# Softmax sums by transposes and a row reduction instead of products with a matrix of ones

## Chip, core and metric

The kernel runs on one core of a Trainium2 chip. The metric is the device time in microseconds of one execution, as the median of several runs. Below, PE is the matrix engine, DVE the vector engine, ACT the scalar engine, POOL the fourth compute engine and SP the queue that starts most transfers. SBUF is the on-chip working memory, PSUM the smaller memory into which PE writes.

## The reference, cut to what matters

One decoder block over 1024 tokens of 1024 features, all in float32: a norm, an input projection, attention with eight heads of 64 beside a state-space mixer, a gated sum of both, and a mixture of 32 experts. The change is in the attention alone:

```python
logits = jnp.einsum('bhqd,bhkd->bhqk', qb, kf) + cb[..., :, None] - cum[:, :, None, :]
causal = pos[None, :] <= pb[:, None]
logits = jnp.where(causal, logits, NEG_INF)
p = jax.nn.softmax(logits, axis=-1)
return jnp.einsum('bhqk,bhkd->bhqd', p, vf)
```

The softmax is computed as exponentials, their product with the values, and at the end a division by the sum of the exponentials over the keys. The change is in how that sum and its reciprocal are made.

## The kernel before

Work on float32 is done by splitting each operand into a high part that PE multiplies at full speed (type fp32r) and the rest, and adding up three products. The stages follow one another: input and state-space projections (0 to 335 us), attention (335 to 655 us), mixing and output projection, routing, and from about 840 us on the experts.

Attention goes by four pairs of heads. For a pair, `proj` (L783) makes queries, keys and values for one half of the tokens, `prep` (L815) turns them and finds row maxima, and `attend(p_, c)` (L871) handles query half `c` (512 queries): for each head `a` of the pair and each block `kt` of 128 keys, PE writes logits with keys on partitions and queries along the columns (L901 to L904), ACT makes the exponentials twice, once rounded to `pH` (L907) and once in full as `pe` (L909), DVE makes the rest `pL` (L910), POOL adds `pe` into `sm` (L912), and PE multiplies both parts with the values into `acc` (L886, L887). `sm` starts as the first block's exponentials. So at the end `sm` is 128 x 512: for each query a column of 128 partial sums, one for each partition. Only blocks up to the diagonal are computed, and the last two blocks of a query half touch only the right 256 columns.

What remains is to add up the 128 partitions and to divide. `sm` is split into `sh` by ACT (L923) and `sl` by DVE (L925). `sel` holds, for each head, a 128 x 128 matrix with ones in that head's 64 columns. Four products of `sel` with `sh` and `sl` of both heads (L930) add up the partitions and leave, in one PSUM tile, the sum of head 0 in partitions 0 to 63 and that of head 1 in 64 to 127. DVE takes the reciprocal in four pieces of 128 columns (L933) and multiplies each with `yu` (L934), which L920 and L921 had brought out of `acc`. Then `yu` is stored (L941), or, for the last half of the last pair, split at once into `yha`, `yla` (L938, L939).

`run_all` (L740) weaves generators by shares: `attend` of the current pair runs beside `proj` and `prep` of the next. For the second half of pair 2 and for pair 3 the filler is `mixed_ssm` (L713), products with the state-space output (L700 to L702), whose results DVE multiplies with gates into `mixS` (L725); ACT makes those gates with another function table (L707), so it loads tables to and fro. The compiler's scheduling layer then sets the order of each engine's queue by its own estimates, so the order of the finished program differs from that of the code; each engine works through its queue in order.

PSUM tiles come from two rings of four: `psA` (`mmtile`, L60), for projections, `acc` and, before, the tile of the sums (except at the last half), and `psB` (`smtile`, L63), for logits, scores and transposes. A tile is taken when the one four places before it in its ring has been read.

Of the kernel before, what the change touches and what calls it, by code (L numbers as in the profile page):

```python
# [10 lines left out]
F32 = mybir.dt.float32  # L11
F32R = mybir.dt.float32r
# [4 lines left out]
ALU = mybir.AluOpType  # L17
AX = mybir.AxisListType

P = 128  # L20
# [22 lines left out]
def hybrid_block(ctx: ExitStack, tc: tile.TileContext, t, out):  # L43

    nc = tc.nc
# [14 lines left out]
    def mmtile():  # L60
        return psA.tile([P, 512], F32, tag="A", name="psA_t")

    def smtile():  # L63
        return psB.tile([P, 512], F32, tag="B", name="psB_t")

    def f32(ap):
        return ap.bitcast(F32)
# [63 lines left out]
    ident = cp.tile([P, P], F32, name="ident")  # L131
# [600 lines left out]
    gev_stack.close()  # L732
    st = ctx.enter_context(ExitStack())
    ap_ = pool(st, "att", 1, side="right")

    sel = ap_.tile([P, 2, P], F32R, name="sel")
    nc.gpsimd.memset(f32(sel), 0.0)
    for a in range(2):
        nc.gpsimd.memset(f32(sel[:, a, a * 64:a * 64 + 64]), 1.0)
    def run_all(*gens):  # L740

        live = [[g, n, lo, hi, 0] for g, n, lo, hi in gens]
# [128 lines left out]
    def attend(p_, c, last=None):  # L871


        nkt = 4 * c + 4
        yu = ap_.tile([P, 512], F32, name="yu", bufs=1)
        sums = []
        for a in range(2):
            kx, qx, ky, qy = p_.KX[a], p_.QX[a, c], p_.KY[a], p_.QY[a, c]

            acc = psA.tile([P, 512], F32, tag="A", name="acc")  # L880
            sm = ap_.tile([P, 512], F32, name="sm", bufs=2)

            def values(kt, o0, n, pH, pL):
                v = p_.V[:, kt, a].rearrange("p a b -> p (a b)")
                o = acc[:, o0:o0 + n]
                nc.tensor.matmul(o, v, pH[:, :n], start=(kt == 0), stop=False)  # L886
                nc.tensor.matmul(o, v, pL[:, :n], start=False, stop=(kt == nkt - 1))  # L887

            late = []
            for kt in range(nkt):  # L890
                ks = slice(kt * P, kt * P + P)
                o0 = max(0, kt * P - c * 512)
                diag = kt >= 4 * c
                if 512 - o0 < 256:
                    o0 -= P
                    d0, dn = 0, 256
                else:
                    d0, dn = 128, 128
                n = 512 - o0
                ps = smtile()  # L900
                nc.tensor.matmul(ps[:, :n], ky[:, ks], qy[:, o0:], start=True, stop=False)  # L901
                if diag:
                    nc.tensor.matmul(ps[:, 0:dn], identb, mask_s[:, d0:d0 + dn], start=False, stop=False)
                nc.tensor.matmul(ps[:, :n], kx[0:68, ks], qx[0:68, o0:], start=False, stop=True)  # L904
                pH = ap_.tile([P, 512], F32R, name="pH", bufs=4)
                pL = ap_.tile([P, 512], F32R, tag="pL", name="pL", bufs=4)
                nc.scalar.activation(pH[:, :n], ps[:, :n], AF.Exp)  # L907
                pe = ap_.tile([P, 512], F32, name="pe", bufs=3) if kt else sm
                nc.scalar.activation(pe[:, :n], ps[:, :n], AF.Exp)  # L909
                nc.vector.tensor_tensor(pL[:, :n], pe[:, :n], f32(pH[:, :n]), ALU.subtract)  # L910
                if kt:
                    nc.gpsimd.tensor_tensor(sm[:, o0:], sm[:, o0:], pe[:, :n], ALU.add)  # L912
                late.append((kt, o0, n, pH, pL))
                if len(late) > 3:
                    values(*late.pop(0))
                yield
            for v in late:
                values(*v)
            orow = slice(a * 64, a * 64 + 64)
            nc.scalar.copy(yu[orow, :], acc[0:64, :])  # L920
            nc.vector.tensor_tensor(yu[orow, :], yu[orow, :], acc[64:128, :], ALU.add)  # L921
            sh = ap_.tile([P, 512], F32R, name="sh", bufs=1)
            nc.scalar.copy(sh, sm)  # L923
            sl = ap_.tile([P, 512], F32R, tag="pL", name="sl", bufs=4)
            nc.vector.tensor_tensor(sl, sm, f32(sh), ALU.subtract)  # L925
            sums += [(a, sh), (a, sl)]
            yield
        ps = smtile() if last is not None else mmtile()
        for j, (a, v) in enumerate(sums):
            nc.tensor.matmul(ps, sel[:, a], v, start=(j == 0), stop=(j == 3))  # L930
        for q in range(4):
            qs = slice(q * P, q * P + P)
            nc.vector.reciprocal(ps[:, qs], ps[:, qs])  # L933
            nc.vector.tensor_tensor(yu[:, qs], ps[:, qs], yu[:, qs], ALU.mult)  # L934
        if last is not None:
            last.append((slot("yha", dt=F32R), slot("yla", dt=F32R)))
            yh, yl = last[-1]
            nc.scalar.copy(yh[:, 512:S], yu)  # L938
            nc.vector.tensor_tensor(yl[:, 512:S], yu, f32(yh[:, 512:S]), ALU.subtract)  # L939
            return  # L940
        nc.gpsimd.dma_start(yaT_d[p_.pr * P:(p_.pr + 1) * P, c * 512:c * 512 + 512], yu)  # L941
# [576 lines left out]
```

## Time and profile before

| | us |
|---|---|
| median of 3 runs | 1182.69 (1181.4 to 1185.41) |
| the profiled execution, its own time | 1180.84 |
| its span, first to last instruction | 1179.2 |
| attention with what is woven in, 340 to 660 | 320.0 |
| PE busy in those 320 us | 306.3 |
| DVE busy | 271.0 |
| ACT busy | 220.6 |
| POOL busy | 168.2 |

PE's busy time is the union of its instructions' durations. Matmuls overlap, so a matmul's duration (0.39 us for 512 columns) is longer than the distance from its start to the next start, which is what one more of them costs. An idle time of PE is shown with what released it. The granted clock is PE's; it is either 2.4 GHz (1.00 in the rows) or half of that, and a stretch with both shows a value between.

### The profile page before, as it was taken

To read this page: it belongs to the slowest core of one execution; us is meant where nothing else is said; L and a number is where in the kernel's file an instruction comes from. 1 tells how busy PE (TensorE), PEld (TensorE's weight loads), DVE (VectorE), ACT (ScalarE), POOL (GpSimd) and SP (SyncE) were. 2 spreads that over 40 slices of the span, in tenths; PEclk is the share of its full clock that TensorE was granted. 3 is DMA by queue.
4 is the path that set the end of the run, shared out by engine and by line. 5 is a ranking of instruction groups with operands and counts; after the bars stand their busy time and mean duration, and the time that the engine had idled before them with its cause. 6 is when DMAs were issued, how large, how long until landed. Compare 5 with 4: busy or idle time off the path is not lost. (4 is left out here: it accounts for less than half of the span.)

```text
span 1179.2 us, 15928 instructions
## 1 busy us (share of the span) xinstructions
PE 1106.0 (94%) x5323; PEld 848.4 (72%) x5324; DVE 804.9 (68%) x1593; ACT 620.3 (53%) x1195; POOL 356.9 (30%) x399
## 2 busy tenths in 40 slices
PE   5999999999999999999899979997699999999995
PEld 4778878887897888788677868885466666666562
DVE  4986887964247899898986795529466666666660
ACT  5443233234246666658868452204376776666662
POOL 3110111013144565647443451102322222222211
PEclk9999999999999999999999999998799999999998
DMA  7625553321604030002523548554599999999992
GB/s 237 88 75 149 130 82 82 81 73 49 152 22 55 11 64 11 16 10 81 205 81 135 184 170 295 181 208 183 188 331 345 327 315 305 314 317 322 311 331 56
DMA packets 100918, 193.78 MB, mean 164 GB/s; under 512 B 26176, under 2 KB 55168, under 8 KB 100832
## 3 DMA queue, kind: packets, MB, share of 16 engines
q1 hardware_dynamic: 82176, 150.16, 41.5%
q0 software_dynamic: 14048, 34.17, 10.6%
q10 hardware_dynamic: 4608, 8.39, 1.9%
q8 instruction: 43, 0.70, 0.2%
q14 instruction: 43, 0.35, 0.1%
HBM read 164.30 MB, written 35.52 MB: 169 GB/s over the span
## 5 line engine op out<-in xcount | busy, mean ns | idle before, releaser
L1104 DVE TENSOR_TENSOR wel<-raw_e,weh 128x512 fp32r<-128x512 f32 x256 | 157.5, 686 | 116.9 <-ACT weh L1103 116.9
L1103 ACT CAST weh<-raw_e 128x512 fp32r<-128x512 f32 x256 | 137.2, 622 | 2.2 <-DVE wel L1104 0.8
L1379 PE MATMUL psA_t<-wd,hT 128*96 128x512 f32 x256 | 115.7, 594 | 3.0 <-DMA wd<-in_w_expert_down 2.2
L912 POOL TENSOR_TENSOR sm<-sm,pe 128x256 f32<-128x256 f32 (+2 forms) x80 | 96.1, 1202 | 70.3 <-ACT pe L909 62.0
L1354 PE MATMUL psA_t<-weh,xh 128*96 128x512 f32 x256 | 103.8, 406 | 0.2
L1355 PE MATMUL psA_t<-wel,xh 128*96 128x512 f32 x256 | 102.2, 399 | 0.0
L1356 PE MATMUL psA_t<-weh,xl 128*96 128x512 f32 x256 | 101.3, 396 | 0.0
L162 PE MATMUL psA_t<-hTl,wgh 128*128 128x512 f32 x256 | 100.7, 393 | 0.0
L161 PE MATMUL psA_t<-hTh,wgl 128*128 128x512 f32 x256 | 100.7, 393 | 0.0
L160 PE MATMUL psA_t<-hTh,wgh 128*128 128x512 f32 x256 | 100.5, 393 | 0.0
L795 PE MATMUL psA_t<-wqh,hTh 128*128 128x384 f32 x256 | 88.0, 344 | 0.0
L796 PE MATMUL psA_t<-wql,hTh 128*128 128x384 f32 x256 | 86.4, 338 | 0.0
L797 PE MATMUL psA_t<-wqh,hTl 128*128 128x384 f32 x256 | 86.3, 337 | 0.0
L1381 POOL DMA_INDIRECT out_rows<-R,ix x32 | 46.0, 1438 | 127.3 <-ACT hT L1370 116.1
L1380 ACT ACTIVATE R<-psA_t,wts 96x512 f32<-96x512 f32 x64 | 43.7, 682 | 75.8 <-PE psA_t L1379 73.7
L1379 PEld LDWEIGHTS psA_t<-wd,hT 128*96 128x96 f32 x256 | 40.0, 167 | 55.0 <-issue 48.9
L1330 POOL DMA_INDIRECT XG<-xn_d,ix x32 | 35.8, 1119 | 139.0 <-PE psB_t L1341 133.1
L907 ACT ACTIVATE pH<-psB_t 128x512 fp32r<-128x512 f32 (+1 forms) x96 | 49.1, 511 | 36.4 <-PE psB_t L904 36.2
L910 DVE TENSOR_TENSOR pL<-pe,pH 128x256 fp32r<-128x256 f32 (+2 forms) x80 | 62.5, 793 | 6.5 <-ACT pe L909 5.7
L164 ACT COPY ge<-psA_t 128x512 f32<-128x512 f32 x32 | 18.7, 584 | 86.6 <-PE psA_t L162 81.8
L857 DVE TENSOR_REDUCE mx<-psB_t 128x1 f32<-128x512 f32 (+2 forms) x96 | 51.2, 551 | 6.2 <-PE psB_t L855 2.7
L1163 PE MATMUL psA_t<-woh,mxh 128*128 128x512 f32 x128 | 54.3, 424 | 1.2 <-DVE gt L988 1.2
(425 smaller groups left out, 2828.7 us busy)
## 6 DMA issues: line engine op xcount, KB each, us to landing
raw_e<-in_w_expert_gate SPq DMA_DIRECT2D x64, 512.0 KB
raw_e<-in_w_expert_up SPq DMA_DIRECT2D x64, 512.0 KB
wd<-in_w_expert_down SPq DMA_DIRECT2D x64, 512.0 KB
gate_d<-ge ACTq DMA_DIRECT2D x32, 256.0 KB
gt<-gate_d SPq DMA_DIRECT2D x16, 512.0 KB
raw_g<-in_w_in SPq DMA_DIRECT2D x12, 512.0 KB
raw_q<-in_w_in SPq DMA_DIRECT2D x48, 128.0 KB
x<-in_x SPq DMA_DIRECT2D x8, 512.0 KB
```

Of the source, the lines that this page charges most:

```text
L160: nc.tensor.matmul(ps, wh, hTh[k][:, ns], start=(k == 0), stop=False)
L161: nc.tensor.matmul(ps, wl, hTh[k][:, ns], start=False, stop=False)
L162: nc.tensor.matmul(ps, wh, hTl[k][:, ns], start=False, stop=(k == KD - 1))
L795: nc.tensor.matmul(ps[:, :384], ah, wh, start=(k == 0), stop=False)
L796: nc.tensor.matmul(ps[:, :384], ah, wl, start=False, stop=False)
L912: nc.gpsimd.tensor_tensor(sm[:, o0:], sm[:, o0:], pe[:, :n], ALU.add)
L1103: nc.scalar.copy(wh[d_], src)
L1104: nc.vector.tensor_tensor(wl[d_], src, f32(wh[d_]), ALU.subtract)
L1354: nc.tensor.matmul(ps, xh[:, k, :], wh[:, k % 2, :], start=(k == 0), stop=False)
L1355: nc.tensor.matmul(ps, xh[:, k, :], wl[:, k % 2, :], start=False, stop=False)
L1356: last = nc.tensor.matmul(ps, xl[:, k, :], wh[:, k % 2, :], start=False, stop=(k == KD - 1))
L1379: pe = nc.tensor.matmul(po, hT[:, j, :], wd[j][:, ns], start=(j == 0), stop=(j == 1))
```

## The change

`sel`, `sh` and `sl` go, with the four products. Instead each head's `sm` is transposed by PE in four pieces of 128 columns into one `psB` tile (L920 of the changed kernel), so that queries lie on partitions, and DVE adds up along each piece's columns into `sums` (L921), 128 x 4 for a head. After both heads DVE takes the reciprocal of the 128 x 8 numbers (L923), ACT writes each 64 times side by side into `rows` (L925), PE transposes `rows` in four pieces back into another `psB` tile (L928), and DVE multiplies that with `yu` in one piece (L929).

```diff
-    sel = ap_.tile([P, 2, P], F32R, name="sel")
-    nc.gpsimd.memset(f32(sel), 0.0)
-    for a in range(2):
-        nc.gpsimd.memset(f32(sel[:, a, a * 64:a * 64 + 64]), 1.0)
...
-        sums = []
+        sums = ap_.tile([P, 4, 2], F32, name="sums", bufs=2)
...
-            sh = ap_.tile([P, 512], F32R, name="sh", bufs=1)
-            nc.scalar.copy(sh, sm)
-            sl = ap_.tile([P, 512], F32R, tag="pL", name="sl", bufs=4)
-            nc.vector.tensor_tensor(sl, sm, f32(sh), ALU.subtract)
-            sums += [(a, sh), (a, sl)]
+
+            ps = smtile()
+            for q in range(4):
+                nc.tensor.transpose(ps[:, q * P:q * P + P], sm[:, q * P:q * P + P], ident)
+            nc.vector.tensor_reduce(sums[:, :, a], ps.rearrange("p (q k) -> p q k", q=4), axis=AX.X, op=ALU.add)
             yield
-        ps = smtile() if last is not None else mmtile()
-        for j, (a, v) in enumerate(sums):
-            nc.tensor.matmul(ps, sel[:, a], v, start=(j == 0), stop=(j == 3))
+        nc.vector.reciprocal(sums, sums)
+        rows = ap_.tile([P, 4, 2, 64], F32, name="rows", bufs=1)
+        nc.scalar.copy(rows, sums.unsqueeze(3).to_broadcast([P, 4, 2, 64]))
+        ps = smtile()
         for q in range(4):
-            qs = slice(q * P, q * P + P)
-            nc.vector.reciprocal(ps[:, qs], ps[:, qs])
-            nc.vector.tensor_tensor(yu[:, qs], ps[:, qs], yu[:, qs], ALU.mult)
+            nc.tensor.transpose(ps[:, q * P:q * P + P], rows[:, q].rearrange("p a f -> p (a f)"), ident)
+        nc.vector.tensor_tensor(yu, ps, yu, ALU.mult)
```

The scheduling layer sets the new order. Three places show it. From L740 up to the changed part of `attend` the line numbers of the changed kernel are five lower.

PE's queue at the end of head 0 in the second query half of pair 2, before (L886 and L887 are the products with the values, L852 and L855 the scores of `prep`, L795 to L797 the projection of the next pair):

```order
L886 MATMUL acc<-pH,V 128x256
L852 MATMUL psB_t<-KX,QX 128x256
L855 LDWEIGHTS identb
L855 MATMUL psB_t<-mask_m,identb 128x128
L795 MATMUL psA_t<-wqh,hTh_137 128x384
L887 MATMUL acc<-pL,V 128x256
L796 MATMUL psA_t<-wql,hTh_137 128x384
```

and with the change:

```order
L881 MATMUL acc<-pH,V 128x256
L882 MATMUL acc<-pL,V 128x256
L920 MATMUL psB_t<-ident,sm 128x128 x4
L847 MATMUL psB_t<-KX,QX 128x256
L850 LDWEIGHTS identb
L850 MATMUL psB_t<-mask_m,identb 128x128
L790 MATMUL psA_t<-wqh,hTh_137 128x384
```

The four transposes of `sm` stand right behind the head's last product, ahead of the scores and the projection, and they need POOL's last addition.

PE's queue at the end of head 1 of the same half, before (L862 turns the maxima of `prep`, L901 to L904 are the logits of pair 3):

```order
L930 MATMUL psA_t<-sh,sel 128x512
L887 MATMUL acc<-pL,V 128x256
L930 MATMUL psA_t<-sl,sel 128x512
L862 MATMUL psB_t<-ident,mx 4x128
L901 MATMUL psB_t<-QY,KY 128x512
```

and with the change:

```order
L920 MATMUL psB_t<-ident,sm 128x128
L882 MATMUL acc<-pL,V 128x256
L920 MATMUL psB_t<-ident,sm 128x128 x3
L928 MATMUL psB_t<-ident,rows 128x128 x4
L857 MATMUL psB_t<-ident,mx 4x128
L896 MATMUL psB_t<-QY,KY 128x512
```

The second transposes follow the first with nothing between, and the next half's logits stand behind them.

DVE's queue at the same place, before (L671 and L684 split loaded operands of the mixing stage):

```order
L921 TENSOR_TENSOR yu<-yu,acc 64x512
L925 TENSOR_TENSOR sl<-sm,sh 128x512
L866 SCALAR_TENSOR_TENSOR ml<-psB_t,mh 4x128
L910 TENSOR_TENSOR pL<-sm,pH 128x512
L933 RECIPROCAL psA_t<-psA_t 128x128
L910 TENSOR_TENSOR pL<-pe,pH 128x384
L934 TENSOR_TENSOR yu<-psA_t,yu 128x128
L684 TENSOR_TENSOR wm<-raw_m,wm 128x512
L933 RECIPROCAL psA_t<-psA_t 128x128
```

and with the change:

```order
L921 TENSOR_REDUCE sums<-psB_t 128x4
L916 TENSOR_TENSOR yu<-yu,acc 64x512
L923 RECIPROCAL sums<-sums 128x8
L671 TENSOR_TENSOR yls<-yrs,yhs 128x1024
L671 TENSOR_TENSOR yla<-yra,yha 128x1024
L929 TENSOR_TENSOR yu<-psB_t,yu 128x512
L861 SCALAR_TENSOR_TENSOR ml<-psB_t,mh 4x128
L905 TENSOR_TENSOR pL<-sm,pH 128x512
```

Four reciprocals and four products, strewn between the next half's `pL`, have become one short reciprocal and one product ahead of them.

In ACT's queue the woven stages of pair 3 come in another order too: the finished program holds 33 loads of function tables where it held 29, all four more of them in that part.

## Rows read from the trace of the kernel before

**Rows 1.** The page, busy time, share of the span and instructions of each engine

```profile
PE 1106.0 (94%) x5323; PEld 848.4 (72%) x5324; DVE 804.9 (68%) x1593; ACT 620.3 (53%) x1195; POOL 356.9 (30%) x399
```

**Rows 2.** Windows: stretch and length; PE, PEld, DVE, ACT, POOL; clock; DMA

```profile
340.00:660.00 320.00, 306.29 (x1625) 254.22 (x1624) 271.02 (x483) 220.55 (x448) 168.20 (x183) 0.99 0.23 64
386.00:400.00 14.00, 13.98 (x79) 12.20 (x78) 12.90 (x26) 8.97 (x21) 7.45 (x9) 1.00 0.01 1
...
528.00:537.00 9.00, 9.00 (x51) 8.00 (x51) 8.65 (x16) 6.39 (x15) 6.83 (x8) 1.00 0.02 6
546.00:590.00 44.00, 38.99 (x197) 30.09 (x197) 42.55 (x68) 35.90 (x67) 23.79 (x22) 1.00 0.50 174
590.00:601.00 11.00, 11.00 (x50) 8.70 (x49) 8.04 (x15) 4.99 (x9) 2.92 (x4) 0.84 0.14 49
601.00:613.00 12.00, 11.43 (x55) 8.49 (x53) 11.91 (x20) 8.33 (x15) 5.06 (x5) 1.00 0.26 87
```

**Rows 3.** Timeline of PE: start, duration, engine, line, operation, tiles, count [idle before]

```profile
645.00 0.40 PE L930 MATMUL psB_t<-sl,sel 128*128 128x512 f32 x1
645.24 0.39 PE L700 MATMUL psA_t<-yha,wm 128*128 128x512 f32 x1
...
398.50 0.60 PE L821 MATMUL psB_t<-ident,qk 128*128 128x128 f32 x4
...
399.29 0.42 PE L901 MATMUL psB_t<-QY,KY 128*128 128x384 f32 x1
399.55 0.23 PE L903 MATMUL psB_t<-mask_s,identb 128*128 128x128 bf16 x1
```

**Rows 4.** Groups by line and form: count, busy us, mean ns, idle before

```profile
L933 DVE RECIPROCAL psA_t<-psA_t 128x128 f32<-128x128 f32 x28 | 26.9, 959 | 1.8 <-PE psA_t L930 1.4
L934 DVE TENSOR_TENSOR yu<-psA_t,yu 128x128 f32<-128x128 f32 x28 | 7.8, 277 | 0.1
L925 DVE TENSOR_TENSOR sl<-sm,sh 128x512 fp32r<-128x512 f32 x16 | 11.3, 706 | 3.7 <-ACT sh L923 3.5
L857 DVE TENSOR_REDUCE mx<-psB_t 128x1 f32<-128x512 f32 x48 | 32.5, 686 | 3.8 <-PE psB_t L852 2.6 <-PE psB_t L855 0.6
L725 DVE TENSOR_TENSOR mixS<-psA_t,gt 128x512 f32<-128x512 f32 x16 | 10.9, 683 | 7.0 <-PE psA_t L702 5.3 <-ACT gt L707 1.7
L388 DVE RECIPROCAL sc<-sc 128x32 f32<-128x32 f32 x1 | 0.3, 332 | 0.0
L923 ACT CAST sh<-sm 128x512 fp32r<-128x512 f32 x16 | 9.9, 620 | 6.8 <-POOL sm L912 6.0 <-PE psA_t L930 0.7
L707 ACT ACT_TABLE_LOAD x7 | 9.0, 1283 | 0.1
L821 PE MATMUL psB_t<-ident,qk 128*128 128x128 f32 x32 | 5.0, 275 | 0.6 <-POOL rstd L809 0.4
```

**Rows 5.** Waits of PE between 340 and 660: total, times, longest

```profile
PE acc L887 <- DVE pL L910: 4.4, 9, 0.9
```

**Rows 6.** Timeline at the end of head 0, second half of pair 2: PE, POOL

```profile
546.05 0.39 PE L887 MATMUL acc<-pL,V 128*128 128x256 f32 x1
546.27 0.34 PE L796 MATMUL psA_t<-wql,hTh 128*128 128x384 f32 x1
...
545.67 2.59 POOL L912 TENSOR_TENSOR sm<-sm,pe 128x256 f32<-128x256 f32 x2
```

**Rows 7.** Timeline at the same place of pair 0: PE, POOL

```profile
407.88 0.34 PE L796 MATMUL psA_t<-wql,hTh 128*128 128x384 f32 x1
408.05 0.36 PE L887 MATMUL acc<-pL,V 128*128 128x256 f32 x1
...
407.66 0.91 POOL L912 TENSOR_TENSOR sm<-sm,pe 128x256 f32<-128x256 f32 x1 [0.93 <-ACT pe L909]
```

**Rows 8.** Timeline of PE after the end of pair 2, and before 590 us

```profile
565.08 0.27 PE L862 MATMUL psB_t<-ident,mx 128*4 128x128 f32 x1
...
589.33 0.50 PE L930 MATMUL psA_t<-sh,sel 128*128 128x512 f32 x1 [1.35 <-DVE mixS L725]
```

## The prediction

> **What bounds the kernel now.** I read the page's busy times first: PE has work for 94% of the span [rows 1]. The change touches attention alone, so the windows of that stage come next: in the 320.0 us from 340 to 660 PE is busy for 306.3, DVE for 271.0, ACT for 220.6 and POOL for 168.2 [rows 2]. So PE leaves 13.7 us idle there, and DVE is the next engine. Work taken from DVE can give back at most what PE loses by waiting for it, and work added to PE's queue counts nearly in full.
>
> Next, where the reciprocals stand. There are eight bursts of four, one behind each half of the queries. Five of them lie in stretches like 386 to 400 and 528 to 537, which are the first and the last of the five: PE is busy for 13.98 of 14 and 9.00 of 9 us, while DVE is busy for 12.90 and 8.65 [rows 2]. There the reciprocals are long but hidden, and PE has matmuls of the projection to go on with. Between 546 and 590 it is otherwise: DVE is busy for 42.55 of 44 us and PE only for 38.99, and the last wait there ends in a result of DVE at 589.33 [rows 2, 8]. From 590 to 601 the granted clock has a mean of 0.84, so for a part of that stretch it was at its lower level, 1.2 GHz, right after PE had sat idle; PE is shown busy all along [rows 2]. From 601 to 613, with the next burst, PE loses 0.57 us. So the burst behind pair 2, and what it delays, is where DVE costs time.
>
> **What goes from PE and what comes.** Products with ones: 32 (four in each of eight halves). Start to start one takes 645.24 - 645.00 = 0.24 us [rows 3]; 32 x 0.24 = 7.7 us. Transposes: 8 heads x 2 halves x 4 = 64 of `sm` and 8 x 4 = 32 of `rows`, 96. The nearest row is the same shape and type in `prep`: eight start at 398.50, and the next matmul starts at 399.29, 0.79 later [rows 3]. That next one, of 384 columns, is followed after 0.26 where such a matmul otherwise takes 408.05 - 407.88 = 0.17 [rows 3, 7], so 0.09 of it belongs to the transposes: 0.88 / 8 = 0.11 us each, 96 x 0.11 = 10.5 us. PE's work grows by 10.5 - 7.7 = **2.8 us**.
>
> A transpose's own duration is 0.275 us [rows 4], but eight of them fit in 0.88, so they overlap. The Trainium skill (TensorE: Matmul & The Clock Gate, Part 4: PE-mode transpose) gives about 275 ns for one transpose in a kernel, mostly access latency; the row's duration agrees with that figure, its distance does not. Priced by that figure the 96 would be estimated at 26.4 us. The sum here goes by the distance; the duration as a price is a rival below.
>
> **What goes from DVE and ACT.** DVE loses 32 reciprocals of 0.96 (30.7 us), 32 products of 0.28 (9.0) and 16 subtractions of 0.71 (11.3), in all 51.0 us. It gets 16 reductions of 512 columns out of PSUM, 0.69 by the score maxima (11.0), 8 products of 512 columns out of PSUM, 0.68 by L725 (5.5), and 8 reciprocals of 8 columns, at most the 0.33 of the one of 32 columns (2.7) [rows 4]: 19.2. So DVE has 31.8 us less to do. Most of this is worth nothing, since five of the eight bursts are hidden. Between 546 and 590 go 3 subtractions, 4 reciprocals and 4 products (7.1 us) and come 3 reductions, one product and one reciprocal (3.1): 4.0 us less in a stretch where DVE is full and PE idles 5.0 us. I take **4.0** as won there, between 0 and 5.0, since the last row before 590 is a wait for DVE. The 0.6 us between 601 and 613 I count as won too. The lower clock cost 0.16 x 11 = 1.8 us; it is won if PE no longer idles before it, and lost again if a new wait of 2 us, below, brings another such stretch. I take 0, with 1.8 to either side.
>
> ACT loses 16 casts of 0.62 (9.9 us) and gets 8 copies of the same size; no row has one that repeats each element, so 0.62 each is the near price (5.0). Four table loads of 1.28 come in [rows 4], between about 568 and 605: 5.1 us. Between 546 and 590 ACT is busy for 35.9 of 44, from 590 to 601 for 4.99 of 11 [rows 2]. So it can fall behind and catch up; I take 0 for them on PE's path, with 5.1 as the upper end. POOL's set-up of `sel` lies ahead of attention, beside PE's work, at nothing.
>
> **What the new waits cost.** Each group of `sm` transposes waits, in PE's queue, for POOL's last addition; before, ACT's cast waited for it, and PE's products with ones stood much later. Behind the transposes stand scores and projection. At the end of head 0 in the second half of pair 2 the last product starts at 546.05 and the next matmul at 546.27, and POOL ends at 545.67 + 2.59 = 548.26 [rows 6]: PE would stand for **2.0 us**. POOL works off a power and a product for `proj` ahead of that addition, and the new order leaves that so. At the same place of pairs 0 and 1 POOL ends at 408.57, and PE reaches the last two transposes, which now stand ahead of the product at 408.05, at about 408.1 [rows 7]: **0.45 each, 0.9** (one of two alike). At the other thirteen ends POOL is done when PE gets there, within a few tenths; I take 0.
>
> `rows` needs a longer round: reduction, reciprocal, ACT's copy, then PE. At seven of the eight ends PE has 13 to 26 rows of other work in its queue between the two groups, 2.9 to 4.5 us by their distances; the round is 0.69 + 0.33 + 0.62 = 1.6 us and up to six other DVE rows of 0.2 to 0.7. So it just fits, at 0; the upper end is about 0.5 each. At the end of pair 2 nothing stands between. With L921's 0.69 in DVE's queue the round is 2.3 us, and the logits, which PE went on to right behind L862 at 565.08 [rows 8], stand behind it: **2.2 us**.
>
> Both long waits, 4.2 us, lie where DVE is full; while PE stands, DVE works off what it has. I take half, **2.1 us**, as covered, between none and all.
>
> **The sum.** 2.8 + 2.0 + 0.9 + 2.2 - 2.1 - 4.0 - 0.6 = +1.2 us. The profiled execution took 1180.84, 1.6 more than its span, so 1182.0 on its own account. The median of the runs, 1182.69, lies 1.85 above it, and the measured time will be a median too: 1182.69 + 1.2 = **1183.9 us**. A measurement of this kernel tells a difference from about 0.3%, 3.5 us; between 1179.1 and 1186.2 it is no change.
>
> **Rivals.**
>
> 1. In-order PE waits: slower. The two long waits are not covered, because what DVE does meanwhile hangs on logits that stand behind them, and so the 4.0 us don't arrive either: 2.8 + 2.0 + 0.9 + 2.2 - 0.6 = +7.3, **1190.0**. Against it speaks DVE's full queue [rows 2], for it that `pL` of the next half comes from just those logits. It decides as soon as less than 3.8 of the 6.1 us (cover and relief) comes. Chance 0.24.
> 2. DVE's relief carries further: faster. An emptier DVE feeds POOL and ACT sooner, so the long waits don't arise, the clock stays up, and the waits for `pL` outside the stretch shrink; all nine come to 4.4 us [rows 5], of which I leave 2.5 for those outside: 2.8 - 4.0 - 0.6 - 1.8 - 2.5 = -6.1, **1176.6**. Against it: POOL's lateness at 546 is its own work. Chance 0.17.
> 3. ACT becomes the bound in pair 3: four table loads and no cover, 1183.9 + 5.1 = **1189.0**. Against it: ACT's idle share after 590. Chance 0.07.
> 4. Transposes cost their own duration on PE: 96 x 0.275 = 26.4 in place of 10.5, **1199.8**. The distances in rows 3 speak against it. Chance 0.02. The figure of the Trainium skill named above would come out in this way.
>
> The forecast itself has 0.50.
>
> **How the numbers follow.** Forecast 0.50 is no change; rivals 1, 3 and 4 (0.33) are slower, rival 2 (0.17) faster. The range goes from 1178.0, a little inside rival 2, to 1191.0, beyond rivals 1 and 3; outside are rival 4 and most of rival 2, with a little of rival 1's upper end (a second clock drop, 1.8): no more than 0.2.
>
> **What would show it.** In the profile after: 96 transposes at 0.11 us from start to start; DVE's busy time in attention down by some 32 us and PE's idle time hardly changed; a wait of PE for `sm` of about 2 us near 546, and one for `rows` of about 2 us near 566; no wait for `mixS` near 589, and perhaps no lower clock behind it. Waits for `rows` at the other seven ends would make the forecast wrong upwards; PE idling less than 8 us in attention would make it wrong downwards.

## The result, and the profile after

The changed kernel takes 1194.7 us (median of six runs, 1188.96 to 1199.33); the kernel before took 1183.08 us in its six runs. The ratio is 1.010, with a 95% interval from 1.0069 to 1.0131: slower by about 12 us, where 1.2 us were forecast and the range ended at 1191.0. The profiled execution after took 1194.5 us (span 1192.6), that of before 1180.84.

The page of the changed kernel, busy time by engine, to be set against [rows 1]; and the costliest group of attention on DVE, whose counterpart of before (62.5 us, 793 ns) is the next line:

```profile
PE 1110.8 (93%) x5387; PEld 853.7 (72%) x5388; DVE 782.8 (66%) x1545; ACT 621.6 (52%) x1191; POOL 355.8 (30%) x396
L905 DVE TENSOR_TENSOR pL<-pe,pH 128x256 fp32r<-128x256 f32 (+2 forms) x80 | 68.9, 872 | 9.9 <-ACT pe L904 8.8
```

```profile
L910 DVE TENSOR_TENSOR pL<-pe,pH 128x256 fp32r<-128x256 f32 (+2 forms) x80 | 62.5, 793 | 6.5 <-ACT pe L909 5.7
```

In the whole span PE is busy for 4.8 us more and DVE for 22.1 us less; PE's figure holds the time that the lower clock adds. The windows of the changed kernel (columns as in [rows 2]: stretch and length, busy PE, PEld, DVE, ACT, POOL, granted clock, DMA) show what that was worth. Attention now ends some 14 us later, so its window is 334 us long:

```profile
340.00:674.00 334.00, 313.67 (x1695) 262.59 (x1694) 251.03 (x435) 221.65 (x445) 168.57 (x183) 0.98 0.23 65
434.20:437.61 3.41, 3.41 (x15) 2.60 (x13) 1.60 (x4) 2.10 (x6) 1.68 (x3) 0.50 0.69 187
553.66:557.07 3.41, 3.16 (x11) 3.07 (x12) 1.36 (x3) 0.00 (x0) 0.19 (x1) 0.50 0.45 154
574.14:580.97 6.83, 4.39 (x18) 2.78 (x16) 4.89 (x8) 3.54 (x7) 3.35 (x6) 0.50 0.49 192
697.03:700.44 3.41, 3.41 (x10) 2.63 (x9) 3.41 (x4) 1.18 (x4) 1.94 (x1) 0.50 0.39 106
546.00:590.00 44.00, 37.60 (x186) 29.80 (x185) 35.48 (x53) 30.59 (x60) 25.01 (x24) 0.88 0.44 154
```

In the stage of attention PE idles 334 - 313.67 = 20.3 us, where it idled 13.7 before [rows 2]. In four stretches the granted clock was at the lower of its two levels, 1.2 GHz (0.50 in the rows); the fourth lies behind that window, among the last products of the mixing stage. What such a stretch costs is half of the time in which PE is busy in it, since a PE that idles loses nothing by its clock: (3.41 + 3.16 + 4.39 + 3.41) / 2 = 7.2 us. Before there was one such stretch of 3.41 us, inside the 11 us of 0.84 in [rows 2], and it cost 1.7 us. Between 546 and 590 DVE is no longer full (35.48 against 42.55), and yet PE does less there than before (37.60 against 38.99).

What PE waits for, from 340 to 675 us (total, times, longest):

```profile
PE psB_t L928 <- ACT rows L925: 5.3, 3, 2.6
PE acc L882 <- DVE pL L905: 4.1, 8, 0.9
PE psB_t L920 <- POOL sm L907: 3.4, 5, 1.6
```

The two new kinds of wait, for `rows` and for `sm`, are 8.7 us; the old one for `pL` is almost what it was [rows 5]. Three places make most of the 8.7.

**The end of head 0, second half of pair 2.** PE, and POOL below the gap (start, duration, engine, line, operation, tiles, count, idle before and what ended it):

```profile
551.88 0.38 PE L920 MATMUL psB_t<-ident,sm 128*128 128x128 f32 x2
553.91 0.69 PE L920 MATMUL psB_t<-ident,sm 128*128 128x128 f32 x2 [1.65 <-POOL sm L907]
...
551.28 2.57 POOL L907 TENSOR_TENSOR sm<-sm,pe 128x256 f32<-128x256 f32 x2
```

This is the place of [rows 6]: two transposes run, the other two stand until POOL's last addition ends at 553.85. A stretch of lower clock begins with it, at 553.66.

**The end of pair 2.** PE, DVE, ACT:

```profile
574.04 1.05 PE L920 MATMUL psB_t<-ident,sm 128*128 128x128 f32 x3
577.48 1.11 PE L928 MATMUL psB_t<-ident,rows 128*128 128x128 f32 x4 [2.39 <-ACT rows L925]
...
575.12 0.69 DVE L921 TENSOR_REDUCE sums<-psB_t 128x4 f32<-128x512 f32 x1 [0.78 <-PE psB_t L920]
575.85 0.69 DVE L916 TENSOR_TENSOR yu<-yu,acc 64x512 f32<-64x512 f32 x1
576.57 0.20 DVE L923 RECIPROCAL sums<-sums 128x8 f32<-128x8 f32 x1
...
576.80 0.62 ACT L925 COPY rows<-sums 128x512 f32<-128x512 f32 x1 [0.92 <-DVE sums L923]
```

The round is as the prediction had it: reduction, another row of 0.69, reciprocal, copy, with nothing on PE between the two groups. The lower clock of 574.14 to 580.97 began before this wait, with the first group still running, and PE's idle time lies inside it.

**The end of pair 0**, which the prediction held to be free. ACT, DVE, PE:

```profile
431.08 0.83 ACT L759 CAST wqh<-raw_q 128x768 fp32r<-128x768 f32 x1 [2.85 <-DMA raw_q<-in_w_in]
433.05 0.62 ACT L925 COPY rows<-sums 128x512 f32<-128x512 f32 x1 [1.14 <-DVE sums L923]
...
429.56 0.69 DVE L921 TENSOR_REDUCE sums<-psB_t 128x4 f32<-128x512 f32 x1
431.95 0.96 DVE L760 TENSOR_TENSOR wql<-raw_q,wqh 128x768 fp32r<-128x768 f32 x1 [1.69 <-ACT wqh L759]
432.82 0.20 DVE L923 RECIPROCAL sums<-sums 128x8 f32<-128x8 f32 x1
...
433.72 0.71 PE L928 MATMUL psB_t<-ident,rows 128*128 128x128 f32 x4 [2.62 <-ACT rows L925]
```

The sums are there at 430.25. The reciprocal that takes 0.20 us starts 2.6 us later, because one row stands ahead of it in DVE's queue, the subtraction that makes `wql` for the next pair. That row waits for ACT's cast of the same weights, and the cast waits for their transfer, `raw_q`. So the chain of the small reciprocals hangs on a transfer of weights with which it has nothing to do, and PE hangs on the chain. The transfer itself landed later too: it was issued at 425.38 and ACT's cast began at 431.08, 5.7 us later, where in the kernel before these were 424.51 and 428.61, 4.1 us apart. No run here shows why it took 1.6 us longer. With the 4.1 us of before, the wait is estimated at 2.6 - 1.6 = 1.0 us.

### The profile page after: what moved, and what is told of

Same layout as the page of the kernel before. It is cut to its first block, busy times and chain, and to the rows that moved or that the text cites. A ratio compares the mean times of both kernels' runs of the same rounds, so it can differ in the third digit from the quotient of the medians.

```text
span 1192.6 us, 15989 instructions
## 1 busy us (share of the span) xinstructions
PE 1110.8 (93%) x5387; PEld 853.7 (72%) x5388; DVE 782.8 (66%) x1545; ACT 621.6 (52%) x1191; POOL 355.8 (30%) x396
## 5 line engine op out<-in xcount | busy, mean ns | idle before, releaser
L905 DVE TENSOR_TENSOR pL<-pe,pH 128x256 fp32r<-128x256 f32 (+2 forms) x80 | 68.9, 872 | 9.9 <-ACT pe L904 8.8
L804 POOL TENSOR_TENSOR rstd<-ss,mhalf 128x4 f32<-128x4 f32 x32 | 35.2, 1101 | 76.3 <-DVE ss L803 32.7
L852 DVE TENSOR_REDUCE mx<-psB_t 128x1 f32<-128x512 f32 (+2 forms) x96 | 50.9, 551 | 10.7 <-PE psB_t L850 5.1
```

## The experiments

Theory W, after the two traces were laid side by side: PE's queue is in order, so the transposes hold up all that stands behind them until POOL's or DVE's and ACT's results are there; the lower clock that follows these waits nearly doubles their price; DVE's relief doesn't come back to PE. (The third stretch began before its wait, as shown above, so that the lower clock follows the waits is a guess here, to be tested.) Rival P: the loss is PE's added work, since 96 transposes cost more than 0.11 us each. Rival S: the waits aren't the cause, they would only move to the next consumer.

Besides the time of the whole kernel I read the length of attention from the profiled execution: from the start of the first product with `pL` (L887 before, L882 after) to the start of the last product with `yla` (L702). It comes out the same in two executions of one kernel: 338.7 and 338.9 below. The second time is the end of the range in rows like these, of before and of after (count, durations in ns min/median/max, first and last start, forms):

```profile
L702 PE MATMUL psA_t<-yla,wm x48: 388/390/398, 645.7 to 691.2; 128*128 128x512 f32 x48
```

```profile
L702 PE MATMUL psA_t<-yla,wm x48: 387/389/628, 657.1 to 705.3; 128*128 128x512 f32 x48
```

The length is then split in three: PE's idle time; what the lower clock cost, as above; and the rest, which is PE's work at the full clock as far as the profile shows it. The windows for that, of before and of after:

```profile
367.10:691.20 324.10, 308.80 (x1591) 253.82 (x1590) 281.99 (x487) 219.43 (x445) 176.76 (x182) 0.99 0.24 76
```

```profile
366.60:705.30 338.70, 316.35 (x1655) 262.21 (x1654) 261.43 (x441) 220.17 (x441) 176.37 (x183) 0.97 0.24 73
```

The ratios are to the kernel before on the same chip.

| run | ratio to before (95%) | median, us | attention, us | PE idle | lower clock | rest |
|---|---|---|---|---|---|---|
| before | 1 | 1183.08 | 367.1 to 691.2: 324.1 | 15.3 | 1.7 | 307.1 |
| the changed kernel | 1.0100 (1.0069 to 1.0131) | 1194.70 | 366.6 to 705.3: 338.7 | 22.3 | 7.2 | 309.2 |
| e5, the same again | 1.0122 (1.0089 to 1.0156) | 1196.71 | 367.7 to 706.6: 338.9 | 23.8 | 5.9 | 309.2 |
| e1, `rows` constant | 1.1936, not comparable | 1409.72 | 366.6 to 700.2: 333.6 | 19.5 | 6.1 | 308.0 |
| e2, `sm` constant | 1.0083, not comparable | 1190.98 | 368.5 to 701.8: 333.3 | 21.1 | 3.9 | 308.3 |
| e3, both constant | 1.1881, not comparable | 1404.89 | 367.5 to 694.1: 326.6 | 14.5 | 5.1 | 307.0 |
| e4, before, short reciprocals | 0.9937, not comparable | 1173.71 | 368.2 to 690.8: 322.6 | 15.4 | 1.7 | 305.5 |
| e6, `rows` later | 1.0060 (1.0032 to 1.0088) | 1188.22 | 368.0 to 703.6: 335.6 | 19.2 | 8.5 | 307.9 |
| e7, both later | 1.0027 (1.0003 to 1.0051) | 1184.88 | 368.0 to 696.7: 328.7 | 17.7 | 3.3 | 307.7 |
| e8, transposes doubled | 1.0222 (1.0182 to 1.0262) | 1207.14 | 366.4 to 716.4: 350.0 | 22.2 | 10.0 | 317.8 |
| e9, e7 with columns of ones | 1.0068 (1.0048 to 1.0089) | 1189.42 | 367.7 to 700.5: 332.8 | 15.6 | 3.1 | 314.1 |
| e13, three raw buffers | 1.0077 (1.0054 to 1.0100) | 1191.63 | 366.9 to 698.7: 331.8 | 19.9 | 3.9 | 308.0 |
| e12, its control | 1.0104 (1.0083 to 1.0125) | 1195.39 | 367.4 to 705.1: 337.7 | 21.2 | 7.2 | 309.3 |
| e14, e7 with three raw buffers | 1.0060 (1.0040 to 1.0080) | 1189.84 | 366.4 to 695.8: 329.4 | 18.6 | 3.4 | 307.4 |

In e1 to e4 the computation is cut, and with other values the experts behind attention get other tokens; so of these four only attention is read, though what was expected of them was put in whole times. PE's work is the same in e4 as before, and the rest differs by 1.6 us; so that column is good to some 2 us.

**e5: are the waits chance?**

> The changed kernel once more, unchanged, for the waits and the stretches of lower clock of a second execution. If the waits of PE belong to the order of the program, they come again at the same places with the same lengths (for rows about 2.6 and 2.4 us, for sm about 1.65 us); if they are chance, they don't. Ratio 1.007 to 1.013.

They come again, at the same places with the same lengths:

```profile
PE psB_t L928 <- ACT rows L925: 5.3, 3, 2.7
PE psB_t L920 <- POOL sm L907: 3.2, 4, 1.6
```

The stretches of lower clock come near the same three places, but not at the same distance: the first begins 1.7 us behind the wait (434.99 to 436.65) where it was 0.5, and the fourth isn't there.

**e1: PE without the wait for `rows`.**

```diff
-            nc.tensor.transpose(ps[:, q * P:q * P + P], rows[:, q].rearrange("p a f -> p (a f)"), ident)
+            nc.tensor.transpose(ps[:, q * P:q * P + P], ident, ident)
```

> The changed kernel, but the 32 transposes that spread the reciprocals read the identity in place of rows (the division by the sums is left out): PE's work is the same, the wait for rows is gone. Theory W (PE's in-order waits and the lower clock behind them are the loss): the waits for rows of 2.62 (433.7), 0.27 and 2.39 us (577.5) go, 5.3 us, and the lower clock at 434.2 to 437.6 and 574.1 to 581.0 (5.1 us) with them: some 10 us less than the changed kernel, ratio to the kernel before near 1.001. Rival P (96 transposes cost PE more than reckoned): PE's work is unchanged, so the time stays near the changed kernel's, ratio 1.008 to 1.012. Rival S (the waits just move to the next consumer of DVE's late results): less than 3 us, ratio above 1.007.

Attention is 5.1 us shorter than in the changed kernel (338.7 to 333.6). That is about the length of the waits (5.3), but only half of the 10 us that were expected. PE's idle time fell by less than the waits, to 19.5 us from 22.3 (23.8 in e5), so a part of them came back as others. The lower clock didn't go with them: it costs 6.1 us here and 7.2 in the changed kernel. The stretch at pair 0 is gone, but from the end of head 0 of pair 2 on there are now three, from 548.83, 569.31 and 579.55, where there were two. So the lower clock doesn't hang on the single wait before it.

**e2: PE without the wait for `sm`.**

```diff
-                nc.tensor.transpose(ps[:, q * P:q * P + P], sm[:, q * P:q * P + P], ident)
+                nc.tensor.transpose(ps[:, q * P:q * P + P], ident, ident)
```

> The changed kernel, but the 64 transposes of the sums read the identity in place of sm (wrong sums; PE's work is the same, the wait of PE for POOL's additions is gone). Theory W: the waits for sm of 1.65 (553.9), 0.58 (408.4) and 0.58 (482.4) us go, 2.8 us, and the lower clock at 553.7 to 557.1 (1.7 us): 4.5 us less than the changed kernel, ratio to the kernel before near 1.006. Rival P: nothing, ratio 1.008 to 1.012. Rival S: under 2 us, ratio above 1.008.

Attention is 5.4 us shorter, where 4.5 were expected.

**e3: both.**

> The changed kernel with both groups of transposes reading the identity: PE waits neither for sm nor for rows, all its work stands, and DVE's and ACT's work too (the division is left out). Theory W: the whole loss goes; what is left is the added PE work of 2.8 us less the relief of DVE of up to 4.6, so 1180 to 1186 us, ratio 0.998 to 1.003. Rival P: stays at 1.007 or above. Rival S: between, 1.004 to 1.008.

12.1 us of attention come back of the 14.6 that the change cost, with the instructions of PE and DVE in place; on ACT two loads of function tables went with the new order (16 in attention, 18 in the changed kernel, 14 before), which may be worth up to 1.0 us (rival 3, below). What is left over before is 326.6 - 324.1 = 2.5 us. That is near the 2.8 of PE's added work, but by luck: the lower clock costs 3.4 us more than before, PE idles 0.8 less, and the rest is the same. Its longest waits of PE, and two windows:

```profile
PE acc L882 <- DVE pL L905: 4.3, 9, 0.9
PE psA_t L701 <- DVE wm L684: 1.7, 1, 1.7
```

```profile
367.50:694.10 326.60, 312.09 (x1656) 261.29 (x1655) 259.90 (x441) 218.11 (x439) 177.57 (x183) 0.98 0.24 76
546.00:590.00 44.00, 39.19 (x194) 31.08 (x195) 39.20 (x57) 32.98 (x61) 22.40 (x22) 0.92 0.49 174
```

No new wait has grown in place of the two, which speaks against S; PE's work alone doesn't make the loss, which speaks against P. The second row says something else as well: even with no wait for `rows` or `sm`, and with a DVE that has 3.4 us less to do there, PE is busy for 39.19 of the 44 us, as before (38.99). The relief of DVE doesn't reach PE.

**e4: the relief of DVE alone, in the kernel before.**

```diff
-            nc.vector.reciprocal(ps[:, qs], ps[:, qs])
+            nc.vector.reciprocal(ps[:, qs][:, 0:8], ps[:, qs][:, 0:8])
```

> The kernel before with reciprocals of 8 columns in place of 128 (most columns are multiplied by the sum, not by its reciprocal: the result is wrong): DVE's relief alone, 32 x (0.96 - 0.3) = 21 us of DVE's work, nothing new on PE. The prediction's step: 2.6 us less between 546 and 590 and 0.6 behind 601, so 1179 to 1180 us, ratio 0.997. If DVE's relief is worth nothing, as in theory W, where PE's own queue and POOL hold it up: ratio 1.000. If it carries further, as the rival with the faster end had it: 1177 us or less, ratio 0.995 or below.

Attention is 1.5 us shorter than before, about half of what the prediction's step gave (3.2 by this kernel's 21 us). The windows of [rows 2] in this kernel:

```profile
546.00:590.00 44.00, 39.71 (x204) 30.82 (x203) 40.93 (x70) 36.65 (x66) 24.27 (x23) 1.00 0.49 174
590.00:601.00 11.00, 10.99 (x56) 8.14 (x56) 10.25 (x21) 5.29 (x11) 3.56 (x6) 1.00 0.19 56
601.00:613.00 12.00, 12.00 (x55) 9.56 (x54) 10.30 (x18) 10.86 (x17) 4.36 (x4) 1.00 0.33 104
```

PE gains 0.7 us between 546 and 590 and 0.6 behind 601, and the lower clock of 590 to 601 doesn't come; one as long comes at 687.18 instead, so over attention the clock costs as much as before. The whole time, 7.3 us below its kernel before, would fit the case in which the relief carries further; but attention ends at 690.8 against 691.2, so nearly all of it lies behind, where the tokens differ. DVE is still busy for 40.93 of 44: where an operation went, the next one moved up.

**e6 and e7: the same transposes, later.** Here the whole computation stands. In e6 the transposes of `rows` and what follows them are put off into the second step of the next half; in e7 those of `sm` too, into the second step of the next head, and `rows` into the fourth step of the next half:

```diff
+    pending = []
...
+                while pending and pending[0][0] <= kt:
+                    pending.pop(0)[1]()
                 yield
...
+            def totals(a=a, sm=sm):
+                ps = smtile()
+                for q in range(4):
+                    nc.tensor.transpose(ps[:, q * P:q * P + P], sm[:, q * P:q * P + P], ident)
...
+            pending.append((1, totals))
...
+        pending.append((1, spread))
+        pending.append((3, finish))
```

`spread` holds the reciprocal and the copy to `rows`, `finish` the transposes of `rows` and all that follows; `pending` is emptied in the steps of `attend`, the number before each name being the step, counted from 0.

> The changed kernel with the result kept: only the four transposes of rows and what follows them are issued later, in the second step of the next half. Theory W: the two long waits for rows (5.0 us) and the lower clock behind them (5.1 us) go, as in the run with constant rows, which won 5.2 us of attention; ratio to the kernel before 1.004 to 1.007. Rival S (the wait moves to another consumer): ratio 1.008 to 1.012. Rival P (PE's work): the same, 1.008 to 1.012.

> The changed kernel with the result kept: the transposes of sm and of rows are both issued later (sm in the second step of the next head, rows in the fourth step of the next half). Theory W: all four kinds of waits go, as in the run with both constant, which kept 2.4 us of attention over the kernel before; ratio 0.999 to 1.004. Rival P: 1.008 or above. Rival S: between, 1.004 to 1.008.

e6 gives 1.006 and e7 1.0027, each inside what theory W expected. e6's interval reaches 1.0088, into the ranges of P and S, so by itself it decides little; e7's ends at 1.0051, clear of P (1.008 or above), and only its upper end lies in the range of S. (e6's profiled execution, at 1194.34 us, was slower than the median of its runs by 6 us, so its attention is longer than its time lets one expect; five stretches of lower clock cost 8.5 us in it.) In e6 one wait for `rows` of 1.2 us is left. In e7 no wait of PE for `sm` or `rows` is left; these are its longest:

```profile
PE acc L884 <- DVE pL L907: 4.9, 9, 1.2
PE psB_t L847 <- ACT pe L906: 3.0, 4, 0.8
PE psB_t L857 <- DVE mx L855: 1.5, 3, 0.5
```

So of the 12 us of the change some 9 are where the transposes stand, not what they cost. The remaining 0.27% is 3.2 us. That is the size of PE's added work, but the trace doesn't put it there: attention is 4.6 us longer than before, of which 2.4 are idle time of PE (the wait of the scores for `pe`, 3.0 us, is not among the waits of the kernel before and 0.6 in the changed one, so S is right in part), 1.6 the lower clock and 0.6 the rest.

**e8: what a transpose costs PE.** Each of the 96 is issued twice.

> The changed kernel with each of the 96 transposes issued twice into the same place: the price of a transpose on PE. At 0.11 us each 10.5 us more than the changed kernel, so some 1205 us, ratio 1.017 to 1.022; at its own duration of 0.275 us 26 us more, ratio 1.032. If PE only filled its waits with them, less than 5 us more, ratio under 1.014.

1207.14 - 1196.71 (e5, on the same chip) = 10.4 us for 96 transposes, 0.109 us each: the 0.11 of the prediction. The runs scatter, and the difference of their means has an interval of 7 to 16 us, 0.07 to 0.16 each; some of it is the lower clock (10.0 us here, 7.2 and 5.9 without), and the rest column has 317.8 - 309.2 = 8.6 us, 0.09 each. Free of that it is to be read from the changed kernel's PE (four of them, then a product of 384 columns that is followed after 0.26 where 0.17 is usual):

```profile
386.35 0.60 PE L920 MATMUL psB_t<-ident,sm 128*128 128x128 f32 x4
386.70 0.42 PE L790 MATMUL psA_t<-wqh,hTh 128*128 128x384 f32 x1
386.96 0.33 PE L791 MATMUL psA_t<-wql,hTh 128*128 128x384 f32 x1
```

(386.96 - 386.35 - 0.17) / 4 = 0.11. The 275 ns that the Trainium skill gives for one transpose (TensorE: Matmul & The Clock Gate, Part 4: PE-mode transpose) is the duration of one, as in [rows 4]. As the price of many in a row it would give an estimate of 26 us here; the run shows 10.4.

**e9: a column of ones in place of the transposes.** If PE's work is what e7 still loses, fewer PE cycles should win it. A product of `sm` with one column of ones gives the sums on the partitions of the queries at once:

```diff
-                    nc.tensor.transpose(ps[:, q * P:q * P + P], sm[:, q * P:q * P + P], ident)
+                    nc.tensor.matmul(ps[:, q:q + 1], sm[:, q * P:q * P + P], ones1, start=True, stop=True)
```

> The version with both groups of transposes issued later, and in it each transpose of sm replaced by a product of the same 128 x 128 piece with one column of ones, which gives the sums themselves on the partitions of the queries (no reduction; reciprocals of 4 columns per head). Result kept. If what that version loses against the kernel before (3.2 us) is PE's work, the time goes with the price of such a product, which no row shows yet: at 0.05 us from start to start 64 x 0.06 = 3.8 us less, ratio to the kernel before near 0.999; at the 0.11 of a transpose nothing on PE, ratio near 1.002; if a product takes several passes, 0.25 or more, 9 us more, ratio 1.010. If the rest is waits instead, the ratio stays at 1.002 to 1.004 whatever the price.

It is slower than e7, 1.0068: 0.41% or 4.8 us more (0.1 to 0.7% by the two intervals; the two ran on different chips). The groups of its weight loads and products show why (count, busy us, mean ns):

```profile
L927 PEld LDWEIGHTS psB_t<-ones,sm 128*128 128x128 f32 x128 | 16.7, 192 | 1.0 <-POOL qk L806 0.3
L927 PE MATMUL psB_t<-ones,sm 128*128 128x1 f32 x128 | 15.2, 239 | 0.0
```

64 products stand as 128 passes, and eight of them take this long (start, duration, then the next row):

```profile
392.89 0.95 PE L927 MATMUL psB_t<-ones,sm 128*128 128x1 f32 x8
393.70 0.42 PE L790 MATMUL psA_t<-wqh,hTh 128*128 128x384 f32 x1
```

0.81 / 8 is at least 0.10 us for a pass with a single column, as much as a transpose with 128 columns. Each pass loads `sm` as weights, and with one moving column little else is left that could set the price. The Trainium skill says that the time of a weight load goes by the number of weight columns, about P / 1.2 ns (TensorE: Matmul & The Clock Gate, LDWEIGHTS (loading the stationary operand)), an estimate of 107 ns for 128; the trace agrees in the distance from start to start (0.10 to 0.11 us), while the row of a load itself lasts 192 ns. 128 x 0.11 in place of 64 x 0.11 is 7 us more on PE, and the rest column has 314.1 - 307.7 = 6.4. The run lost 4.8, less than that: PE idles 2.1 us less than in e7, as 16 reductions of 0.69 also went from DVE.

**e10 to e13: is it the late weights?** Three buffers for the raw weights instead of two, `rows` sharing the buffers of `pe` to make room; the control does the second alone.

```diff
-            raw = wq.tile([P, 2, 3, P], F32, name="raw_q", bufs=2)
+            raw = wq.tile([P, 2, 3, P], F32, name="raw_q", bufs=3)
...
-        rows = ap_.tile([P, 4, 2, 64], F32, name="rows", bufs=1)
+        rows = ap_.tile([P, 4, 2, 64], F32, tag="pe", name="rows", bufs=3)
```

> The changed kernel with three buffers for the raw weights in place of two (rows shares the buffers of pe to make room): the weights for the last cast at the end of pair 0 can be fetched earlier. Theory W, with the queue as the reason for the wait of 2.6 us near 434 (the reciprocals stand behind a subtraction of weights whose transfer is late): that wait falls below 1 us, and the lower clock behind it goes, 3 to 4 us less than the changed kernel; the waits near 554 and 578 stay. Ratio to the kernel before 1.006 to 1.009. If the wait comes from the round of reduction, reciprocal and copy itself, it stays above 2 us, ratio 1.010 to 1.013.

> The changed kernel with rows in the buffers of pe, and two buffers for the raw weights as before: what the sharing alone does. The wait near 434 stays at 2.4 to 2.8 us; time as the changed kernel's, 1190 to 1198 us.

> The changed kernel with rows in the buffers of pe and two buffers for the raw weights, timed beside the same with three. Theory W: the wait of 2.8 us near 434 is there; ratio to the kernel before 1.008 to 1.013, and 3 to 4 us above the kernel with three buffers on the same chip. If the late weights cost the whole kernel nothing (the gain is given back behind attention): less than 1.5 us above it.

> The changed kernel with three buffers for the raw weights, again, beside its control on the same chip. Theory W: no wait for rows above 1 us near 434; ratio to the kernel before 1.005 to 1.009, 3 to 4 us below the control. If the gain is given back behind attention: within 1.5 us of the control.

With three buffers DVE's rows at the end of pair 0 follow one another without a stop, and the reciprocal runs right behind the reduction (e10):

```profile
428.11 0.94 DVE L760 TENSOR_TENSOR wql<-raw_q,wqh 128x768 fp32r<-128x768 f32 x1
...
430.08 0.69 DVE L921 TENSOR_REDUCE sums<-psB_t 128x4 f32<-128x512 f32 x1
430.81 0.20 DVE L923 RECIPROCAL sums<-sums 128x8 f32<-128x8 f32 x1
```

PE's wait for `rows` in e10 (in the control e11 it is 5.5 us, three times, the longest 2.8):

```profile
PE psB_t L928 <- ACT rows L925: 2.4, 1, 2.4
```

Of the three waits for `rows` only that of pair 2 is left. On one chip the kernel with three buffers takes 1191.63 us (e13) and its control 1195.39 (e12): 3.8 us, inside the 3 to 4 that were expected (the difference of the means of six runs each has an interval of 0.8 to 5.8 us). Attention is 5.9 us shorter, 3.3 of it by the lower clock, so some 2 of that are given back behind it; two table loads went here too. e10 itself took 1190.07 (1.0067, 1.0043 to 1.0091), e11 1191.97 in a single run. The third buffer also let three rows of DVE's queue change places there, so it is the earlier transfer with that order that was tested, not the transfer alone.

**e14: is there a version that beats the kernel before?** e7 with three raw buffers.

> Both groups of transposes issued later, and three buffers for the raw weights (rows in the buffers of pe): is there a version of this change that beats the kernel before? Theory W: no wait for sm or rows is left for the third buffer to remove, and PE's added work of 2.8 us stays, so the ratio to the kernel before stays at 1.000 to 1.004. If late weights also hold up pL and the scores: 1 to 3 us better, 0.998 to 1.001.

No: 1.006, where 1.000 to 1.004 was expected. Its attention is as long as e7's (329.4 against 328.7), so the buffer won nothing there; its interval and e7's (to 1.0051) overlap, and what lies behind attention I have not traced. None of the versions beats the kernel before.

## Why the prediction was wrong, point by point

- **PE's work, +2.8: right as far as can be read.** Rows give 0.11 us a transpose, e8 0.07 to 0.16, and the rest column grows by 2.1 us, good to some 2. The 2.5 us of e3 and the 3.2 of e7 are of the same size by luck: most of each is lower clock and idle time.
- **Waits for `sm`, +2.0 and +0.9: right in place and nearly in size.** 1.65 us at 553.91 in place of 2.0; 0.58 each at 408.37 and 482.41 in place of 0.45; two more, taken as 0, make the 3.4 full.
- **Wait for `rows` at the end of pair 2, +2.2: right.** 2.39 us.
- **Waits for `rows` at the other seven ends, 0 with at most 0.5 each: wrong at one of them.** At the end of pair 0 it was 2.62 us, at the end of pair 1 0.27. The step reckoned the round by the durations of "up to six other DVE rows of 0.2 to 0.7"; it didn't ask what those rows wait for. One of them, the subtraction for `wql`, stood waiting for ACT, and ACT for a transfer. In the trace of before the subtraction (L765) is there too, between 429.85 and 430.79, ahead of the reciprocals (L933); they could wait, as nobody on PE waited for them soon. The change made a reciprocal that nobody waited for into one that PE waits for, and with that the whole queue ahead of it. That the transfer took 1.6 us longer than before is part of the 2.62 and stays open. e13 against e12 shows 3.8 us for this wait and what comes with it.
- **Cover, -2.1: didn't come.** It was reckoned that DVE works off its queue while PE stands. It did, and then ran dry, since the scores that feed it stood behind PE's transposes:

```profile
558.37 0.56 DVE L852 TENSOR_REDUCE mx<-psB_t 128x1 f32<-128x384 f32 x1 [2.71 <-PE psB_t L850]
```

- **DVE's relief, -4.0 and -0.6: too large.** PE's idle time in attention grew by 22.3 - 15.3 = 7.0 us and the two new waits are 8.7, so 1.7 us of the older waits went; the wait for `mixS` near 589 [rows 8] is no longer in the list, as foretold. e4 bounds it from the other side, with nothing new on PE: 0.7 + 0.6 us, and 1.5 in all of attention. That DVE was full for 42.55 of 44 us made it look like the limit of that stretch; but PE there waits for one thing after the other, and the next was late by nearly as much. The count of DVE's rows was right: 51.1 us went and 18.1 came, 33.0 in place of 31.8. But DVE's busy time in attention fell by only 271.02 - 251.03 = 20.0 us, in a window 14 us longer, and by 22.1 in the whole span. Of what is missing there, 6.4 us is the subtraction for `pL`, which takes that much longer now for the same 80 rows (68.9 against 62.5).
- **Clock, 0 with 1.8 to either side: wrong.** 7.2 us lost against 1.7, so 5.5 more. A stretch at 1.2 GHz lay at each of the three long waits, twice at about its end and once from before it (in e5 up to 1.7 us later), and a fourth near the end of attention. The prediction allowed for one such stretch in place of another. What brings each is not settled: with the waits for `rows` gone (e1) 6.1 us were lost, with both kinds gone 5.1 in e3 and 3.3 in e7.

With the measured terms: PE's work 2.1, the new waits 8.7, the older waits -1.7, the clock 5.5, in all 14.6 us, by which attention grew. This is how the growth divides, and no proof of the terms, as PE's work is what is left when the others are taken off. The largest errors are the clock (5.5 for 0), cover and relief (1.7 for 6.7) and the wait at the end of pair 0 (2.62 for 0). The whole profiled execution grew by 13.7, the median by 12.0; runs of the same kernel differ by up to 10 us after the change, and what the stages behind attention gave back I read from no row.

Rival 1 was the right mechanism. It was to decide as soon as less than 3.8 of the 6.1 us of cover and relief came, and 1.7 came. It gave 1190.0, 4.7 us short, since it too held the end of pair 0 free and the clock unchanged. Rival 4, the transposes by their own duration, is out. Rival 3, the four table loads, was there in small: they came (33 in place of 29), and one wait of PE stands behind two of them in ACT's queue, which has no gap from 593.07 on:

```profile
596.75 1.28 ACT L902 ACT_TABLE_LOAD   x1
599.93 1.14 ACT L683 CAST wm<-raw_m 128x512 fp32r<-128x512 f32 x2
...
600.60 0.50 PE L700 MATMUL psA_t<-yhs,wm 128*128 128x512 f32 x1 [1.03 <-ACT wm L683]
```

Before, this wait was 0.3 us. So the rival is worth at most 1.0 us of the 5.1 it put down. No run took the table loads away by themselves; with two fewer, in e1, e3, e7 and e13, this wait is gone.

## What to carry to other kernels

A consumer on an in-order engine should be issued where its operand has long been made: the same 96 transposes cost 12 us right behind their producers and 3 us a step or two later (7 in e14, which also has the third buffer). When a change lets a fast engine wait for a small operation on another, the price isn't that operation's duration but everything queued ahead of it there, with what that waits for, down to a transfer of unrelated weights; so each row of the queue is to be followed to its own releaser. And work taken from a full engine is worth only what the engine behind it idles for that reason alone: 22 us of DVE's time were worth about 2 on PE, and 21 us in e4 1.5.

## What the runs showed of the hardware

- **PE's idle time came with nearly as much lower clock.** 7.0 us more of it came with 5.5 us more lost to the lower clock (in e5, 8.5 with 4.2). It isn't paid wait by wait (e1, above), and e6 lost 8.5 us with less idle time than the changed kernel. When all new waits went in e7, the stretch around the end of pair 2 had one short piece left, at a mean of 0.66 over 5 us, and another came at 686.71:

```profile
570.00:575.00 5.00, 4.54 (x21) 3.37 (x21) 4.00 (x8) 4.69 (x10) 4.52 (x5) 0.66 0.97 375
```

- **A single-precision product with one moving column costs two passes, each as dear as a transpose** (e9): 0.11 us from start to start, by its weight load as far as the run shows.
- **An emptier DVE ran slower.** The subtraction for `pL` has two operands in SBUF and takes 0.68 us for 512 columns undisturbed; its mean over all shapes rose from 793 to 872 ns, and in e4, where only DVE's reciprocals were cut, these rows took 66.7 us in all. In the trace the long ones, up to 2 us, all lie beside POOL's work; none without it took more than 0.7. The Trainium skill says that GpSimd shares its SBUF interfaces with VectorE and contends with instructions that have two SBUF inputs (GPSIMD Engine Reference, 1. Specifications). The trace agrees with that, but some rows of 0.68 do so too, and no run here takes POOL's additions away; so it stays argued, not shown.
